# A hybrid decoder trunk: side tasks held back by VectorE's queue, and one small product in rounded form

## The chip, the cores and the metric

The kernel runs on one core of a Trainium2 chip. The metric is the device time of one execution in microseconds; the time given for a kernel is the median of several runs. A profiled execution, taken on the same core, gives the trace. Engines: TensorE (PE, with its weight loads PEld), VectorE (DVE), ScalarE (ACT), GpSimd (POOL) and SyncE (SP, which issues the DMAs).

## The reference

One layer over 256 tokens of 1024 channels. A normalised, conditioned `h` goes through one wide input projection; three mixers work on its parts (a matrix memory with a short convolution, a 31-tap convolution module, and a sparse attention), their outputs go through a projection each, are weighted by sigmoid gates and summed, and an output projection and a norm end it. The change touches the attention. Cut to that:

```python
def compress(t, j):                      # 15 blocks of 32 tokens, stride 16
    blk = ...                            # (15, G_C, 32 * 128), plus pe[j]
    return gelu(blk @ w1[j]) @ w2[j]
kc, vc = compress(k_cmp, 0), compress(v_cmp, 1)
# per block of queries, G_C = 2 groups of 4 heads:
s_c = einsum('bqgjd,bngd->bgjqn', qb, kc) * scale
p_c = masked_softmax(s_c, cmp_end <= t)
o_c = einsum('bgjqn,bngd->bqgjd', p_c, vc)      # the product that the change rewrites
... # o_s (selected blocks), o_w (window) likewise over 256 keys
return gb0 * o_c + gb1 * o_s + gb2 * o_w
```

## The kernel before

**Numbers.** The large products are done with float32 split in two rounded halves: `w_hi` is the weight cast to the rounded type `F32R` on ScalarE, `w_lo` the rest, subtracted on VectorE. A projection is three products, hi x hi, lo x hi and hi x lo. Smaller products, the attention's among them, run in plain float32.

**Order.** The kernel is written out once, in program order, by a planner (`Loom`, lines 74 to 250), which keeps for each engine the time until which it has given it work (`free`), with modelled costs. The main line issues TensorE's projections: `group_feat` (256 columns, output `ps_f`) and `tok` (512 columns, `ps_t`, two banks out of a ring of three). After every few matmuls it calls `weave` (line 206). That steps side tasks, which are Python generators: each runs to its next `yield`, which gives the planned time at which it may go on. Tasks have ranks: 0 for the weight splits, 1 for what the main line will want soon (the short convolutions, the heads of the matrix memory, the gates' sigmoids), and 2, the default of `spawn` (line 225), for the others: `u_gen`, the compression (`cmp_gen`), the small gates (`misc_gen`), the attention (`nsa_gen`, line 919), the tails of two branches (`branch_a`, line 1230, with `num` and `ga`; `branch_b`, line 1239, with `lsum`, `u` and `lsq`) and the output gate (`gate_gen`, line 712, with `a_raw`). The 31-tap convolution is the fill (line 212): it is stepped while VectorE's planned queue is under 600 ns beyond TensorE's position. `need` (line 232) forces a task to its end at once; the main line does so with the attention before the `cz` projections (line 1209), with each branch before its product (line 1287), and with the output gate before the last projection (line 1308).

**The weights' way.** Four raw buffers of 1 MB each are filled by DMA; side tasks that load (the compression and the output gate) take one of the four while they work.

**The attention's sum.** For each of 2 groups and 2 halves of the tokens, `nsa_gen` computes scores (`ps_s`), exponentials (`pm`), and scales them; `flips` (line 1002) then transposes the probabilities by blocks of 128 keys into a bank `pt` (`ps_p`), and copies it to `p_t`. For the 16 compressed keys it copies 16 rows to `ptc`, a tile whose other 112 rows were set to zero, and the product takes `vcmp[g]`, a tile filled in the same way by the compression (line 811), as its weights. All blocks are summed in one bank, `ps_o`, which is copied to `oc`.

**The branches' end.** After the `cz` projections the main line computes the gate of a branch (`mix_gate`, line 1258: `tok`, then VectorE adds a bias into `gs`), then the branch's product, in the order c, a, b.

Of the kernel before, what the change touches and what calls it, by code (L numbers as in the profile page):

```python
# [11 lines left out]
F32 = mybir.dt.float32  # L12
F32R = mybir.dt.float32r
AF = mybir.ActivationFunctionType
OP = mybir.AluOpType
# [52 lines left out]
RAWS, HIS, LOS = 4, 3, 3  # L68
GAP = 600.0
SLACK = 250.0  # L70
ROOM = dict(act=900.0, dve=900.0)


class Loom:
# [58 lines left out]
    def until(self, engine, *aps):  # L133
        return max(self.when(engine, a) for a in aps) + (SLACK if engine == "pe" else 0.0)

# [64 lines left out]
    def room(self, engine):  # L200
        return self.free[engine] - ROOM[engine]

# [2 lines left out]

    def weave(self):
        while True:
            task = next((t for t in self.tasks if t[0] <= self.now()), None)
            if task is None:
                break  # L210
            self.step(task)
        while self.fill and self.free["dve"] < self.now() + GAP:
            self.step(self.fill[0])
            if self.fill[0][2]:
                self.fill.pop(0)
# [49 lines left out]
def trunk(ctx: ExitStack, tc, xtok, crow, wada, wave0, wgrp, wmisc, w1, wbr, wout, par, vbias, out):  # L265
    nc = tc.nc
    const = ctx.enter_context(tc.tile_pool(name="const", bufs=1))
# [10 lines left out]
    act, dve, pe = [Line(loom, e, n) for e, n in ((nc.scalar, "act"), (nc.vector, "dve"), (nc.tensor, "pe"))]  # L278
    pool = nc.gpsimd
    until, weave, spawn, need, drop = loom.until, loom.weave, loom.spawn, loom.need, loom.drop  # L280
# [4 lines left out]
    def midt(name, shape):  # L285
        return mid.tile(shape, F32, name=name, tag="mid")
# [4 lines left out]
    def bank(name, kind="mm"):  # L291
        return loom.alloc(psum.tile([128, 512], F32, name=name, tag=kind, bufs=BANKS[kind]), kind, BANKS[kind])
# [10 lines left out]
    def flip(o, a):  # L303
        return pe.transpose(o, a, ident)
# [22 lines left out]
    def pc(name, i=0, n=1):  # L327
        return p_sb[:, PAR[name] + i:PAR[name] + i + n]
# [408 lines left out]
    ckv = ckb[:, 0].rearrange("p (a b c) -> p a b c", a=2, b=2)  # L737
    kk = [const.tile([128, 528], F32, name=f"kk{g}") for g in range(2)]
    vtok = midt("vtok", [128, 2, 2, 256])
    vcmp = [const.tile([128, 128], F32, name=f"vcmp{g}") for g in range(2)]  # L740
    for g in range(2):
        pool.memset(vcmp[g], 0.0)

    def cmp_gen(j):
        for g in range(2):
            c = ckv[:, j, g, :]
            src = bass.AP(tensor=c.tensor, offset=c.offset, ap=[list(c.ap[0]), [1, 32], [16, 15]])
            dve.tensor_tensor(blk[:, :, 16 * g:16 * g + 15], src,
                              pc("pe", 32 * j, 32)[:, :, None].broadcast_to([128, 32, 15]), op=OP.add)
        yield from loom.slot("sd")  # L750
        ps = bank("ps_c1", "sd")

        def load(c):
            w = rawt([128, 8, 256], "w1_raw")
            loom.load(nc.sync, w, w1[4 * j + c])
            return w

        yield from raw_slot()
        nxt = load(0)
        for c in range(4):  # L760
            if c < 3:
                yield from raw_slot()
            w, nxt = nxt, load(c + 1) if c < 3 else None
            yield until("pe", w, blk)
            for e in range(8):
                q = e % 4
                mm(ps[32 * q:32 * q + 32, 0:256], blk[:, 8 * c + e, :], w[:, e], c == 0 and e < 4,
                   c == 3 and e >= 4, tile_position=(0, 32 * q), skip_group_check=True)
            raw_free(w)
        part = ringt(work, [128, 256], "part", "mu", 1)  # L770
        yield until("act", ps)
        act.copy(part, ps[:, 0:256])
        drop(ps)
        yield until("pe", part)
        yield from loom.slot("sd")
        ps = bank("ps_c2", "sd")
        for f in range(2):
            mm(ps[:, 32 * f:32 * f + 32], part[:, 128 * f:128 * f + 128], gather4, True, True)
        hid = work.tile([128, 64], F32, name="hid", tag="hid")
        yield until("act", ps)  # L780
        act.copy(hid, ps[:, 0:64])
        drop(ps)
        yield until("dve", hid)
        t = work.tile([128, 64], F32, name="gt", tag="gt")
        dve.tensor_tensor(t, hid, hid, op=OP.mult)
        dve.tensor_tensor(t, t, hid, op=OP.mult)
        dve.scalar_tensor_tensor(t, t, 0.044715, hid, op0=OP.mult, op1=OP.add)
        yield until("act", t)
        act.activation(t, t, AF.Tanh, scale=0.7978845608028654)
        yield until("dve", t)  # L790
        dve.tensor_scalar(t, t, 0.5, 0.5, op0=OP.mult, op1=OP.add)
        dve.tensor_tensor(hid, hid, t, op=OP.mult)
        yield until("pe", hid)
        w2 = [pc("w2", (2 * j + f) * 128, 128) for f in range(2)]
        if j == 0:
            yield from loom.slot("sd")
            ps = bank("ps_kc", "sd")
            for f in range(2):
                mm(ps[:, 0:32], w2[f], hid[:, 32 * f:32 * f + 32], f == 0, f == 1)
            yield until("act", ps)  # L800
            for g in range(2):
                act.copy(kk[g][:, 384:400], ps[:, 16 * g:16 * g + 16])
            drop(ps)
        else:
            for g in range(2):
                yield from loom.slot("sd")
                ps = bank("ps_vc", "sd")
                for f in range(2):
                    mm(ps[0:16, 0:128], hid[:, 32 * f + 16 * g:32 * f + 16 * g + 16], w2[f], f == 0, f == 1)
                yield until("act", ps)  # L810
                act.copy(vcmp[g][0:16, :], ps[0:16, 0:128])
                drop(ps)

    blk = ckb[:, 1].rearrange("p (a b) -> p a b", a=32)
# [104 lines left out]
    def nsa_gen(qs, oc, ptc):  # L919
        for g in range(2):  # L920
            for t in range(2):
# [62 lines left out]
                if t == 0:  # L984
                    full = [pc_, pm[:, :, 0:128], pm[:, :, 128:256]]
                else:
# [3 lines left out]
                    full = [pc_, pm[:, :, 0:256], w]  # L990
# [11 lines left out]
                def flips(c, kind, kt):  # L1002
                    w = 16 if kind == 2 else 128
                    yield from loom.slot("sd")
                    pt = bank("ps_p", "sd")
                    for j in range(4):
                        flip(pt[0:w, 128 * j:128 * j + 128], pm[:, j, c:c + w])
                    yield until("act", pt)
                    if kind == 2:
                        act.copy(ptc[0:16, :], pt[0:16, :])  # L1010
                        drop(pt)
                        return vcmp[g], ptc
                    p_t = ringt(work, [128, 512], "p_t", "p_t", 2)
                    act.copy(p_t, pt)
                    drop(pt)
                    return vtok[:, kt, kind, 128 * g:128 * g + 128], p_t
# [107 lines left out]
    for n, ev in (("cks", evac_kk(True)), ("ckw", evac_kk(False))):  # L1124
        group_feat(n, 0, ev)
    group_tok("cv", 0, lambda t, ps: dve.tensor_tensor(vtok[:, t].rearrange("p a b -> p (a b)"), ps, vb_kv[:, 0:512],
                                                       op=OP.add))
# [1 line left out]
    for i in range(4):  # L1129
        group_feat("cq", i, evac_fn(lambda t: qs[:, t]))  # L1130
    oc = bigt("oc")
    ptc = const.tile([128, 512], F32, name="ptc")
    pool.memset(ptc, 0.0)

    def nsa_all():
        yield from loom.after(g_cmp, g_misc)
# [325 lines left out]
```

## Time and profile before

| | us |
|---|---|
| median of 3 runs | 511.48 (511.13 to 512.28) |
| profiled execution, its own time | 511.16 |
| its span | 509.4 |
| PE busy | 497.6 (98%) |
| PEld busy | 440.4 (86%) |
| DVE busy | 434.7 (85%) |
| ACT busy | 310.9 (61%) |

The span goes from the first instruction to the last; the time has a little more around it. Busy shares are averages over stages with different limits. Matmuls overlap in TensorE, so its busy time says less than the distance between the starts of neighbouring matmuls. A releaser, written `<-DVE gs`, is the engine and tile whose end let the instruction begin. Mean granted clock of TensorE over the span: 0.995 of its full speed.

### The profile page before, as it was taken

What the parts mean: (1) busy time and instruction counts of PE and PEld (TensorE: products, weight loads), DVE (VectorE), ACT (ScalarE), POOL (GpSimd) and SP (SyncE); (2) the same over time, 40 slices, a digit from 0 to 9 for tenths busy, and PEclk for the clock granted to TensorE, in tenths of its full rate; (3) what the DMA queues carried; (4) which work ended last, traced back from release to release, by engine and by line L of the source; (5) the groups of instructions that cost most, each with busy time, mean ns of one, the idle gap of its engine ahead of it and who ended that gap; (6) DMA issues with size and microseconds to landing.
All of it is one profiled execution on the core that took longest, in us unless ns stands there. A gap on an engine that the chain in (4) does not pass through costs nothing.

```text
span 509.4 us, 8567 instructions
## 1 busy us (share of the span) xinstructions
PE 497.6 (98%) x3258; PEld 440.4 (86%) x3258; DVE 434.7 (85%) x876; ACT 310.9 (61%) x524; POOL 7.3 (1%) x40
## 2 busy tenths in 40 slices
PE   8999999999999999999999999998999999999994
PEld 6999999799878989888898999996878888888883
DVE  4999799999999899899899987679998975756755
ACT  5656756335465858979497775666566844354442
POOL 4000000000000000000000000000000000000000
PEclk9999999999999999999999999998999999999999
DMA  7999954884774234404324247544657685455402
GB/s 262 382 406 356 406 223 156 330 323 167 279 300 167 95 154 160 170 8 167 134 109 167 84 144 271 206 166 165 224 182 297 247 314 215 174 196 215 169 0 82
DMA packets 18042, 105.32 MB, mean 207 GB/s; under 512 B 2129, under 2 KB 2257, under 8 KB 7890
## 3 DMA queue, kind: packets, MB, share of 16 engines
q1 hardware_dynamic: 18002, 104.79, 55.3%
q8 instruction: 25, 0.41, 0.3%
q14 instruction: 15, 0.12, 0.1%
HBM read 103.73 MB, written 1.05 MB: 206 GB/s over the span
## 4 chain that ended last, share of the span: by engine, by line
PE 91%; DVE 5%; DMA 1%; issue 1%; ACT 1%; DVEq 0%; SPq 0%; ACTq 0%
PE ps_f L165 35%; PE ps_t L165 29%; PE w L165 9%; PE ps_out L165 4%; PE ps_o L165 3%; PE ps_s L165 2%; PE ps_c L165 2%; DVE w_lo L165 1%; PE ps_p L165 1%; DMA x_sb<-in_xtok_dram 1%; PE ps_qk L165 1%; PE ps_n L165 1%; DVE u L165 1%; PE ps_heat L165 1%; DVE lsum L165 0%
## 5 line engine op out<-in xcount | busy, mean ns | idle before, releaser
L165 DVE TENSOR_TENSOR w_lo<-w_raw,w_hi 128x1024 fp32r<-128x1024 f32 x148 | 180.3, 1221 | 39.3 <-ACT w_hi L165 39.1
L165 ACT CAST w_hi<-w_raw 128x1024 fp32r<-128x1024 f32 x148 | 154.7, 1046 | 81.5 <-PE ps_t L165 55.0
L165 PE MATMUL ps_f<-h_hi,w_hi 128*128 128x256 f32 x512 | 131.0, 292 | 0.0
L165 PE MATMUL ps_f<-h_lo,w_hi 128*128 128x256 f32 x512 | 126.1, 283 | 0.0
L165 PEld LDWEIGHTS ps_f<-h_hi,w_hi 128*128 128x128 f32 x512 | 98.0, 191 | 2.9 <-issue 2.4
L165 PEld LDWEIGHTS ps_f<-h_lo,w_hi 128*128 128x128 f32 x512 | 98.1, 192 | 1.4 <-issue 1.0
L165 DVE SCALAR_TENSOR_TENSOR acc<-u,p_sb,acc 128x226 f32<-128x226 f32 (+28 forms) x232 | 93.1, 461 | 0.9 <-ACT acc L165 0.9
L165 PE MATMUL ps_f<-h_hi,w_lo 128*128 128x256 f32 x512 | 76.4, 288 | 0.0
L165 PEld LDWEIGHTS ps_f<-h_hi,w_lo 128*128 128x128 f32 x512 | 67.2, 191 | 2.0 <-issue 1.3
L165 PE MATMUL ps_t<-w_hi,h_hi 128*128 128x512 f32 x144 | 57.3, 398 | 2.0 <-DVE gs L165 2.0
L165 PE MATMUL ps_t<-w_hi,h_lo 128*128 128x512 f32 x144 | 56.6, 393 | 0.0
L165 PE MATMUL ps_t<-w_lo,h_hi 128*128 128x512 f32 x144 | 45.9, 400 | 0.0
L165 PEld LDWEIGHTS ps_t<-w_hi,h_hi 128*128 128x128 f32 x144 | 27.4, 190 | 8.3 <-DVE gs L165 2.5
L165 ACT ACT_TABLE_LOAD x25 | 32.1, 1283 | 1.2 <-PEq L1454 0.8
L165 PEld LDWEIGHTS ps_t<-w_lo,h_hi 128*128 128x128 f32 x144 | 26.9, 190 | 6.2 <-issue 0.8
L165 PEld LDWEIGHTS ps_t<-w_hi,h_lo 128*128 128x128 f32 x144 | 27.4, 190 | 5.4
L165 PE MATMUL w<-h_lo,w_hi 128*128 128x256 f32 x128 | 31.4, 283 | 0.0
L165 PE MATMUL w<-h_hi,w_lo 128*128 128x256 f32 x128 | 31.4, 283 | 0.0
L165 DVE SCALAR_TENSOR_TENSOR a_raw<-a_raw,cb 128x1024 f32<-128x1024 f32 x24 | 28.6, 1219 | 0.0
L165 PEld LDWEIGHTS w<-h_hi,w_lo 128*128 128x128 f32 x128 | 24.6, 192 | 0.0
L165 PEld LDWEIGHTS w<-h_lo,w_hi 128*128 128x128 f32 x128 | 24.6, 192 | 0.0
L165 ACT ACTIVATE pm<-pm,mx 128x16 f32<-128x16 f32 (+2 forms) x48 | 19.0, 401 | 0.3 <-DVE mx L165 0.3
(261 smaller groups left out, 707.8 us busy)
## 6 DMA issues: line engine op xcount, KB each, us to landing
w_raw<-in_wgrp_dram SPq DMA_DIRECT2D x50, 1024.0 KB, 4.8
w_raw<-in_wbr_dram SPq DMA_DIRECT2D x12, 1024.0 KB, 4.8
a_raw<-in_wada_dram SPq DMA_DIRECT2D x16, 512.0 KB, 6.8
w_raw<-in_wave_dram SPq DMA_DIRECT2D x16, 512.0 KB, 6.7
w_raw<-in_w_dram SPq DMA_DIRECT2D x8, 1024.0 KB, 4.8
a_raw<-in_wada_dram SPq DMA_DIRECT2D x4, 1024.0 KB, 4.8
w_raw<-in_wout_dram SPq DMA_DIRECT2D x4, 1024.0 KB, 4.8
vb_mg<-in_vbias_dram SPq DMA_DIRECT2D x3, 512.0 KB, 6.6
```

The source lines that it names most:

```text
L165: inst = self.pin(fn(*args, **kw))
```

## The change

First, `weave` no longer takes a task of rank 2 while the planner's VectorE is given work beyond 1500 ns after TensorE's position; tasks of rank 0 and 1, the fill and `need` are not affected. Second, the product of the compressed keys' probabilities with the compressed values is done with rounded operands, as one product. The rows of `vcmp` hold, at partitions 0, 32 and 64, the rounded values twice and their rest; those of `ptc` hold the rounded probabilities, their rest, and the rounded probabilities again. One product over all 128 partitions thus sums hi x hi, hi x lo and lo x hi. ScalarE writes the rounded copies (two instead of one), VectorE subtracts the rest out of the PSUM bank, and the task has a `yield` for VectorE in between.

```diff
+BACKLOG = 1500.0
@@ weave
-            task = next((t for t in self.tasks if t[0] <= self.now()), None)
+            full = self.free["dve"] > self.now() + BACKLOG
+            task = next((t for t in self.tasks if t[0] <= self.now() and not (full and t[3] == 2)), None)
@@
-    vcmp = [const.tile([128, 128], F32, name=f"vcmp{g}") for g in range(2)]
+    vcmp = [const.tile([128, 128], F32R, name=f"vcmp{g}") for g in range(2)]
     for g in range(2):
-        pool.memset(vcmp[g], 0.0)
+        pool.memset(vcmp[g].bitcast(F32), 0.0)
@@ cmp_gen
                 yield until("act", ps)
-                act.copy(vcmp[g][0:16, :], ps[0:16, 0:128])
+                for q in (0, 32):
+                    act.copy(vcmp[g][q:q + 16, :], ps[0:16, 0:128])
+                yield until("dve", vcmp[g])
+                dve.tensor_tensor(vcmp[g][64:80, :], ps[0:16, 0:128], vcmp[g][0:16, :], op=OP.subtract)
                 drop(ps)
@@ flips
                     if kind == 2:
-                        act.copy(ptc[0:16, :], pt[0:16, :])
+                        for q in (0, 64):
+                            act.copy(ptc[q:q + 16, :], pt[0:16, :])
+                        yield until("dve", ptc)
+                        dve.tensor_tensor(ptc[32:48, :], pt[0:16, :], ptc[0:16, :], op=OP.subtract)
                         drop(pt)
                         return vcmp[g], ptc
@@
-    ptc = const.tile([128, 512], F32, name="ptc")
-    pool.memset(ptc, 0.0)
+    ptc = const.tile([128, 512], F32R, name="ptc")
+    pool.memset(ptc.bitcast(F32), 0.0)
```

## Rows read from the trace of the kernel before

**Rows 1.** The page's busy time, share of the span and instructions of each engine.
```profile
PE 497.6 (98%) x3258; PEld 440.4 (86%) x3258; DVE 434.7 (85%) x876; ACT 310.9 (61%) x524; POOL 7.3 (1%) x40
```
**Rows 2.** Chain of waits, then TensorE in time: start us, us, what.
```profile
183.48 0.86 PE ps_o L165 x2
...
338.35 0.40 PE L165 MATMUL ps_t<-w_hi,h_hi 128*128 128x512 f32 x1
338.58 0.40 PE L165 MATMUL ps_t<-w_hi,h_lo 128*128 128x512 f32 x1
```
**Rows 3.** Who waited for whom: us in total, times, longest us.
```profile
PE ps_t L165 <- DVE gs L165: 2.0, 1, 2.0
...
PEld ps_o L165 <- ACT ptc L165: 0.2, 1, 0.2
```
**Rows 4.** Windows: length, busy of PE, PEld, DVE, ACT, POOL; clock, DMA share, GB/s.
```profile
351.70:353.75 2.05, 0.01 (x2) 0.00 (x1) 2.05 (x4) 0.66 (x2) 0.00 (x0) 1.00 0.35 68
353.75:357.27 3.52, 3.52 (x11) 2.85 (x11) 3.52 (x6) 2.70 (x4) 0.00 (x0) 0.52 0.62 258
...
357.27:379.20 21.93, 21.93 (x106) 18.22 (x105) 20.69 (x32) 13.93 (x18) 0.00 (x0) 1.00 0.60 216
...
388.00:454.00 66.00, 66.00 (x301) 54.93 (x300) 48.66 (x58) 36.92 (x46) 0.00 (x0) 1.00 0.61 231
```
**Rows 5.** Groups by form on ScalarE and VectorE: busy us, mean ns, idle before.
```profile
L165 ACT COPY ptc<-ps_p 16x512 f32<-16x512 f32 x4 | 2.3, 563 | 0.0
...
L165 ACT COPY vcmp<-ps_vc 16x128 f32<-16x128 f32 x2 | 0.5, 252 | 1.5 <-PE ps_vc L165 1.5
...
L165 DVE TENSOR_TENSOR cm<-cm 4x256 f32<-4x256 f32 x7 | 2.9, 413 | 0.2
...
L165 DVE TENSOR_TENSOR m_lo<-ps_mf,m_hi 128x512 fp32r<-128x512 f32 x4 | 2.7, 686 | 0.4 <-ACT m_hi L165 0.4
```
**Rows 6.** TensorE, then VectorE in time around the wait for `gs`.
```profile
348.83 0.39 PE L165 MATMUL ps_t<-w_hi,h_hi 128*128 128x512 f32 x1
...
351.10 0.61 PE L165 MATMUL ps_t<-w_lo,h_hi 128*128 128x512 f32 x2
...
348.36 1.22 DVE L165 TENSOR_TENSOR w_lo<-w_raw,w_hi 128x1024 fp32r<-128x1024 f32 x1
349.50 0.68 DVE L165 TENSOR_TENSOR ga<-ps_ht,ga 128x512 f32<-128x512 f32 x1
350.10 0.73 DVE L165 TENSOR_SCALAR num<-num,mv,hf__4126 128x256 f32<-128x256 f32 x2
350.75 1.21 DVE L165 TENSOR_TENSOR w_lo<-w_raw,w_hi 128x1024 fp32r<-128x1024 f32 x1
351.88 1.21 DVE L165 TENSOR_TENSOR u<-u,mu 128x1024 f32<-128x1024 f32 x1
353.02 1.27 DVE L165 TENSOR_TENSOR gs<-ps_t,vb_mg 128x512 f32<-128x512 f32 x2
```
**Rows 7.** Tile `ya_lo` (durations ns, first and last start us); the page's weight loads.
```profile
L165 PEld LDWEIGHTS ps_t<-w_hi,ya_lo x32: 187/188/192, 400.7 to 434.2; 128*128 128x128 f32 x32
...
L165 DVE TENSOR_TENSOR ya_lo<-ga,ya_hi x4: 684/686/687, 370.7 to 381.1; 128x512 fp32r<-128x512 f32 x4
...
w_raw<-in_wgrp_dram SPq DMA_DIRECT2D x50, 1024.0 KB, 4.8
```
**Rows 8.** VectorE's groups from 158 to 283; the attention's end and `cz`'s start in time.
```profile
L165 DVE SCALAR_TENSOR_TENSOR acc<-u,p_sb,acc 128x248 f32<-128x248 f32 (+28 forms) x102 | 40.8, 459 | 0.0
L165 DVE TENSOR_TENSOR w_lo<-w_raw,w_hi 128x1024 fp32r<-128x1024 f32 x30 | 36.5, 1217 | 1.0 <-ACT w_hi L165 1.0
...
267.19 2.35 DVE L165 TENSOR_TENSOR pm<-pm,sm 128x1024 f32<-128x1024 f32 x2
...
281.08 0.59 ACT L165 COPY oc<-ps_o 128x512 f32<-128x512 f32 x1
...
315.31 0.28 PE L165 MATMUL ps_f<-h_hi,w_hi 128*128 128x256 f32 x1
```

## Prediction

> **What bounds the kernel now.** I read the shares of busy time first, then who waited for whom on TensorE, then tables of short windows around each wait, and last the instructions in order of time there. TensorE (PE) is busy for 497.6 of 509.4 us [rows 1], VectorE (DVE) for 85%. A busy share alone could mislead, so look at the starts: two 512-column products of rounded (fp32r) operands start 0.23 us apart [rows 2], and the next ones follow without a gap. TensorE is therefore the bound nearly everywhere, and time is won in only two ways: by giving it less to do, or by closing a hole. After the start-up there is one hole worth the name: TensorE waited once for 2.0 us on VectorE's `gs` [rows 3]. In the window of that wait, 351.70 to 353.75, TensorE did 0.01 us of work while VectorE was busy without a break; in the 3.52 us behind it the granted clock was 0.52, the lower of the two levels (1.2 GHz), and it is 1.00 again from 357.27 on [rows 4]. The hole thus costs 2.05 us of standing still, and 3.52 x (1 - 0.52) = 1.69 us of slow work: 3.7 us.
>
> A rule of the Trainium skill speaks against this reading: "Perfetto Trace Analysis", Identifying the Most-Contended Engine, says that matmul busy time is no measure of TensorE's headroom, and that the busy share of weight loads should be taken beside the useful work. By that, 86% would leave 14% of the span as room, and a saving on one product could vanish in it. The starts 0.23 us apart, product after product, agree with the first reading and not with this one: an engine with room would leave gaps. By the one reading the sum is the one below, by the other it is rival B.
>
> **Part 2, the compressed keys' product with the values.** It runs four times (2 groups x 2 token halves). Each is a float32 product of 512 columns that appears as two records and takes 0.86 us on the chain of waits [rows 2]. After the change it is one rounded product of the same 512 columns over all 128 partitions (the unused ones hold zeros, as before); 512 columns of that kind take 0.23 us. Saved: 4 x (0.86 - 0.23) = 2.5 us of TensorE. As nothing but TensorE's own work ends these stretches, I count all of it. Bounds: 0 if the place is filled by a new wait, 2.5 if not; I take 2.5.
>
> Added on ScalarE (ACT): a second copy of 16x512, four times at 0.56 us, and a second of 16x128, twice at 0.25 us: 2.7 us [rows 5]. Added on VectorE: four subtractions 16x512 out of PSUM into a rounded tile. The trace has none with 16 partitions; the nearest is `m_lo`, the same operands on 128 partitions, 0.69 us. Few partitions don't make it much cheaper: 4x256 still takes 0.41 us, over half of that for half the columns. So 4 x 0.69 and two of 128 columns at 0.4 or less: 3.5 us; bounds 1.6 us (the 4x256 price four times, nothing for the small ones) and 3.6 us. What hides both: ScalarE is busy 61% of the span, and on VectorE the work displaces convolution steps, a fill that runs only when nothing else is queued. If that cover were gone, the 3.5 us would stand in front of splits, as a further 3.5 us of holes at most. New wait: the product waits for VectorE's subtraction rather than ScalarE's copy. Behind it on TensorE stand the projections `ps_f`; a misjudged VectorE would hold them, perhaps 0.5 us each time, 0 to 2 us for four. I take 0, since the planner places a TensorE instruction 250 ns after the operand is due, and the product waited for ScalarE's `ptc` only 0.2 us in all four rounds [rows 3]. The two memsets change only the type under which they are written; no DMA is added or moved.
>
> **Part 1, the gate on low-rank tasks.** Before, any side task whose due time has come is stepped at each pause of the matmuls. Now one of rank 2 (the default: the compression, the small gates, the attention, the two branch tails, the output gate) isn't stepped while the planner has over 1.5 us of VectorE work queued beyond TensorE's position. Ranks 0 (weight splits) and 1, the fill, and everything forced by `need` go on. Look at the hole. The first bank of the gate product was complete when the last six matmuls began at 348.83; TensorE needs that bank back after those of 351.10, about 351.7. The evacuation `gs` reads as many columns as `m_lo` (0.69 us), so it should start by 351.0; it starts at 353.02 [rows 6]. In front of it, behind the split already running, VectorE does `ga` (0.60, by the distance of the starts), `num` (0.65), a split `w_lo` (1.13), and `u` minus the mean (1.14). Three of the four are rank 2, of the branch tails: 2.39 us. VectorE's backlog then is 353.02 - 348.83 = 4.2 us, far above 1.5, so these are what the gate holds. Without the three, `gs` starts at 350.6, is done at 351.3, and the hole is gone, with the clock's drop: 3.7 us gained. If only the last is held, it starts at 351.9 and the hole is 0.9 us. But the gate lets a step through at any backlog below 1.5, and one step can bring 1.1 us more (as `u` does), and a split 1.14 on top. So the queue met by `gs` lies between 1.5 and 3.8 us; it may reach 2.2 (351.0 - 348.83) without harm. The ends are 0 and 3.7 us gained; below nothing, the same hole might come twice, 3.7 us lost. I take 3.3: the hole shrinks to where TensorE shows no drop, with 0.4 us left over.
>
> What is late next: the held work moves into 357 to 379, where VectorE is 94% busy (20.69 of 21.93), so the gate will stay near its threshold there, and then past 388, where it has 66 - 48.7 = 17 us of room [rows 4]. Branch a's last `ya_lo` starts at 381.1, and its product's weight loads begin at 400.7 [rows 7]: 19 us to give away for some 5 us of held work. The output gate's task holds one of four raw buffers while it waits, which leaves three for the weights; a load of 1 MB lands in 4.8 us [rows 7] and feeds 24 products, 24 x 0.23 = 5.5 us.
>
> **Sum.** Against the profiled execution: 511.16 - 2.5 - 3.3 = 505.4 us. The median of the three runs is 0.3 above that execution, so 505.7.
>
> **Rivals.**
> A, the hole stays or moves. For it: 94% busy VectorE right behind, and steps that pass at 1.4 us; against it: 2.4 us of the 4.2 in front of `gs` is of the gated kind. Time 511.5 - 2.5 = 509.0, down to 507 with half a hole. The gate doing nothing, because the planner never sees its backlog, gives the same 509.0.
> B, TensorE has hidden room and the rounded product saves nothing; the hole still goes: 511.5 - 3.3 = 508.2.
> C, slower: the attention comes late. It is rank 2, and from 158 to 283 VectorE is full: 30 splits take 36.5 us and 102 convolution steps 40.8 us [rows 8]. The fill stops near 0.6 us (its own bound) plus a pair of steps at 0.46 us, so at 1.5, just at the threshold; each split laid on it can close the gate for its own length: at most 36.5 us in all. To that comes the longer chain of part 2, 4 x (0.56 + 0.69 + about 1 us of queue) = 9 us. The last copy into `oc` starts at 281.08, and the attention is forced to its end where the `cz` projections begin, at 315.31: 33.6 us to spare. I expect a third of the bound, 12 + 9 = 21 us, so it holds. Past 34 us of delay, the last round's chain (from its last scaling at 267.2 to 281.7, 14 us, of which TensorE itself needs some 6 for five products at 0.86 and its transposes) runs with nothing beside it: 8 us of hole, with 1.7 us at the lower clock behind it as above. Time 509.0 + 9 or 10 = 518.5, or 515 if the first hole goes all the same.
> D, no change: smaller new holes (the product's wait, buffers held longer by paused tasks) eat the gain: 511.5.
>
> **Chances.** The forecast 0.52, its own range 503.6 to 507; A 0.22; B 0.05; C 0.13; D 0.08. What can be told from no change here is 0.2%, 1.0 us. Faster: 0.52 + 0.22 + 0.05 = 0.79; same: 0.08; slower: 0.13. The range begins at 503.6 (both terms whole, 511.5 - 2.5 - 3.7 = 505.3, less the 1.0 us by which a measurement may be off and some shorter waits) and goes to 511.5, which takes in A, B and half of D.
>
> **What would show it.** Right: four single records of `ps_o<-ptc,vcmp` of about 0.4 us with 0.23 us to the next start; no TensorE wait on `gs` above 0.5 us and a granted clock of 1.00 near 350; `lsum`, `num`, `u` later than before, `gs` within 2 us of its bank. Wrong: a wait on `gs` or `merged` of 1 us or more anywhere from 335 to 400 (A); a TensorE span that shrinks by less than the records saved (B); a hole at the start of `cz`, with `oc` or `pm` as its releaser (C); TensorE waiting on `ptc`, or weight loads waiting on a DMA (D).

## The result: slower by 0.6%

The changed kernel takes 515.0 us (514.7 to 515.5) against 511.7 us of the kernel before, run beside it: a ratio of 1.0064, 95% interval 1.0048 to 1.0081. The prediction had 505.7 and a range to 511.5, so it was wrong in sign. The profiled execution took 514.95 us, its span is 513.2.

The page's busy line of the changed kernel stands almost as in [rows 1]: TensorE works as long as before, in a longer span.

```profile
PE 497.1 (97%) x3254; PEld 441.0 (86%) x3254; DVE 438.3 (85%) x882; ACT 309.3 (60%) x526; POOL 7.3 (1%) x40
```

Who waited for whom on TensorE (us in total, times, longest) shows a changed picture. The hole at `gs` of [rows 3] is gone as forecast. In its place stand two waits for a weight split `w_lo`, which the kernel before did not have, and two for `ptc`.

```profile
PE ps_f L166 <- DVE w_lo L166: 5.4, 2, 4.0
PE ps_o L166 <- DVE ptc L166: 1.3, 2, 0.9
...
PE ps_t L166 <- DVE gs L166: 0.2, 1, 0.2
```

The steps of the small product: ScalarE's casts, VectorE's subtraction, the product (durations in ns, least, median, most, then first and last start).

```profile
L166 ACT CAST ptc<-ps_p x8: 559/574/577, 186.9 to 316.9; 16x512 fp32r<-16x512 f32 x8
L166 DVE TENSOR_TENSOR ptc<-ps_p,ptc x4: 680/680/680, 188.9 to 318.3; 16x512 fp32r<-16x512 f32 x4
...
L166 PE MATMUL ps_o<-ptc,vcmp x4: 391/498/499, 189.7 to 319.0; 128*128 128x512 f32 x4
```

The product has four records of 0.39 to 0.50 us, where [rows 2] had two records and 0.86 us for each. The subtraction takes 0.680 us on 16 partitions, nearly the 0.686 of 128 in [rows 5]. So the price of each step by itself was near.

To see where the time went, cut the execution at two marks: the first and the last start of the projections `ps_f`, and the last start of the output product `ps_out`. They stand in the tiles' first and last starts; the last copy into `oc` is the end of the attention.

```profile
L166 PE MATMUL ps_f<-h_hi,w_hi x512: 278/283/682, 62.4 to 345.0; 128*128 128x256 f32 x171
...
L166 PE MATMUL ps_f<-h_hi,w_lo x512: 277/283/582, 64.3 to 346.1; 128*128 128x256 f32 x171
```

```profile
L166 PE MATMUL ps_out<-w_hi,m_lo x32: 388/389/397, 483.8 to 505.9; 128*128 128x512 f32 x32
```

The same in the kernel before:

```profile
L165 PE MATMUL ps_f<-h_hi,w_hi x512: 278/283/682, 61.6 to 337.2; 128*128 128x256 f32 x171
...
L165 PE MATMUL ps_f<-h_hi,w_lo x512: 274/283/682, 63.5 to 338.2; 128*128 128x256 f32 x171
...
L165 PE MATMUL ps_out<-w_hi,m_lo x32: 388/389/397, 480.0 to 502.1; 128*128 128x512 f32 x32
```

And the copies into `oc` in the changed kernel:

```profile
L166 ACT COPY oc<-ps_o x4: 562/577/588, 192.4 to 319.5; 128x512 f32<-128x512 f32 x4
```

The first stretch, 62.4 to 346.1, is 283.7 us; before it was 276.6 (61.6 to 338.2). The last, to 505.9, is 159.8 us; before it was 163.9. So the change lost 7.1 us in the first and won 4.1 us in the last; 0.8 us more passed before the first stretch began, in these two executions. The attention ends at 319.5; before it ended at 281.1 [rows 8].

The loss in the first stretch lies around the two waits for `w_lo` (windows: length, busy time of PE, PEld, DVE, ACT, POOL; granted clock, DMA share, GB/s).

```profile
293.85:295.26 1.41, 0.00 (x0) 0.00 (x0) 1.41 (x3) 1.40 (x3) 0.00 (x0) 1.00 0.00 0
298.40:302.36 3.96, 0.00 (x0) 0.00 (x1) 3.73 (x9) 1.09 (x2) 0.00 (x0) 0.75 0.00 0
302.36:307.20 4.84, 4.84 (x22) 4.84 (x23) 4.84 (x7) 1.72 (x3) 0.00 (x0) 0.50 0.79 247
307.20:340.00 32.80, 32.78 (x254) 30.21 (x253) 26.91 (x48) 18.88 (x28) 0.00 (x0) 1.00 0.48 173
```

In 1.41 and 3.96 us TensorE did nothing, and in the 4.84 us behind the second its clock was 0.50, the lower level (1.2 GHz), as behind the old hole in [rows 4]. What VectorE and ScalarE did there, in order of time (start, us, what; in brackets the idle time ahead of it and what ended it):

```profile
287.34 1.04 ACT L166 CAST w_hi<-w_raw 128x1024 fp32r<-128x1024 f32 x1
288.39 1.28 ACT L166 ACT_TABLE_LOAD   x1
289.69 0.63 ACT L166 ACTIVATE ga<-ga 128x512 f32<-128x512 f32 x1
...
290.80 0.36 ACT L166 COPY num<-ps_n 128x256 f32<-128x256 f32 x1
291.18 1.28 ACT L166 ACT_TABLE_LOAD   x1
292.47 0.51 ACT L166 ACTIVATE pm<-pm,mx 128x256 f32<-128x256 f32 x1
...
293.09 1.28 ACT L166 ACT_TABLE_LOAD   x1
```

```profile
291.19 0.43 DVE L166 BATCH_NORM_STATS2 st<-ps_n 128x6 f32<-128x256 f32 x1 [4.32 <-ACT num L166]
...
291.76 2.31 DVE L166 SCALAR_TENSOR_TENSOR acc<-u,p_sb,acc 128x236 f32<-128x236 f32 x6
293.99 1.22 DVE L166 TENSOR_TENSOR w_lo<-w_raw,w_hi 128x1024 fp32r<-128x1024 f32 x1
295.13 3.12 DVE L166 SCALAR_TENSOR_TENSOR acc<-u,p_sb,acc 128x239 f32<-128x239 f32 x8
298.16 0.22 DVE L166 TENSOR_TENSOR pm<-pm,keep 128x64 f32<-128x64 f32 x1
...
301.09 1.22 DVE L166 TENSOR_TENSOR w_lo<-w_raw,w_hi 128x1024 fp32r<-128x1024 f32 x1
```

On ScalarE the last exponentials of the late attention (`pm`) alternate with the heads' activations (`ga`, `zb`, `sz`), and each change of function brings a table load of 1.28 us: three from 288.39 to 294.37. The copy `num` of the matrix memory stands in that queue until 290.80. VectorE's next instruction in its queue, the statistics `st`, needs `num`: VectorE stands for 4.32 us. What is queued behind it comes late: six convolution steps, a split (first hole), eight steps and the attention's scaling (`pm`, `sm`), and only at 301.09 the split that ends the second hole. The table loads themselves are not more than before: four start between 280 and 325 us in either kernel (21 in the whole span, 25 before). New are the exponentials: four of them stand on ScalarE between this copy of `num` and the one ahead of it (284.95), none between the same two copies before. There VectorE waited 1.7 us for `num`.

### The profile page after: what moved, and what is told of

The parts are those of the page before. It is cut to its first block, busy times and chain, and to the rows that moved or that the text cites. A ratio compares the mean times of both kernels' runs of the same rounds, so it can differ in the third digit from the quotient of the medians.

```text
span 513.2 us, 8574 instructions
## 1 busy us (share of the span) xinstructions
PE 497.1 (97%) x3254; PEld 441.0 (86%) x3254; DVE 438.3 (85%) x882; ACT 309.3 (60%) x526; POOL 7.3 (1%) x40
## 4 chain that ended last, share of the span: by engine, by line
PE 81%; DVE 9%; DMA 5%; ACT 3%; issue 2%; SPq 0%; DVEq 0%; ACTq 0%
PE ps_f L166 32%; PE ps_t L166 30%; PE w L166 5%; PE ps_out L166 4%; DMA w_raw<-in_wave_dram 4%; DVE w_lo L166 3%; PE ps_s L166 2%; DVE acc L166 2%; PE ps_c L166 2%; PE ps_o L166 2%; DMA x_sb<-in_xtok_dram 1%; PE ps_p L166 1%; PE ps_qk L166 1%; ACT w_hi L166 1%; PE ps_n L166 1%
## 5 line engine op out<-in xcount | busy, mean ns | idle before, releaser
L166 ACT ACT_TABLE_LOAD x21 | 26.9, 1283 | 1.1 <-PEq L1462 0.8
```

Of the source, the lines that this page charges most:

```text
L166: inst = self.pin(fn(*args, **kw))
```

## The experiments

All times are medians; each ratio is to the kernel before, run beside it. First stretch, last stretch and the start of the last `oc` copy are read in each trace as above.

| run | us | ratio to before (95%) | first | last | `oc` |
|---|---|---|---|---|---|
| before | 510.8 to 511.7 | | 276.6 | 163.9 | 281.1 |
| changed | 515.0 | 1.0064 (1.0048-1.0081) | 283.7 | 159.8 | 319.5 |
| e1 product only | 519.2 | 1.0152 (1.0133-1.0171) | 284.0 | 164.3 | 306.3 |
| e2 gate only | 509.1 | 0.9952 (0.9938-0.9966) | 278.5 | 159.8 | 305.8 |
| e3 attention free | 513.6 | 1.0048 (1.0032-1.0064) | 282.5 | 159.9 | 304.3 |
| e4 attention held | 520.3 | 1.0176 (1.0158-1.0194) | 284.9 | 165.7 | 320.0 |
| e5 product placed later | 515.8 | 1.0088 (1.0073-1.0103) | 280.2 | 164.4 | 308.0 |
| e6 no rest | 511.6 | 1.0012 (1.0003-1.0022) | 276.9 | 164.3 | 296.3 |
| e7 tails held | 507.2 | 0.9925 (0.9912-0.9937) | 276.7 | 159.8 | 280.7 |
| e8 statistics later | 513.6 | 1.0054 (1.0039-1.0069) | 283.2 | 159.8 | 317.3 |
| e9 work only | 518.2 | 1.0142 (1.0125-1.0160) | 279.8 | 166.6 | 299.7 |
| e10 first term only | 511.6 | 1.0007 (0.9999-1.0016) | 274.7 | 166.3 | 292.6 |
| e11 same, old order | 510.8 | 0.9992 (0.9980-1.0004) | 276.3 | 163.9 | 281.2 |
| e12 tails held, flips early | 513.4 | 1.0045 (1.0030-1.0060) | 283.8 | 159.8 | 313.9 |
| e13 tails held, work only | 511.5 | 1.0023 (1.0002-1.0044) | 279.7 | 159.8 | 300.5 |
| e14 tails held, first term | 505.6 | 0.9895 (0.9882-0.9908) | 274.7 | 159.8 | 293.5 |
| e15 tails held, product | 515.0 | 1.0071 (1.0059-1.0083) | 283.8 | 159.8 | 305.6 |
| e16 tails held, subtractions | 509.1 | 0.9960 (0.9948-0.9972) | 278.6 | 159.8 | 299.3 |
| e17 tails held, attention late | 507.4 | 0.9929 (0.9917-0.9942) | 276.7 | 159.8 | 294.7 |
| e18 tails held, later still | 514.4 | 1.0067 (1.0055-1.0078) | 283.8 | 159.8 | 324.1 |

### Which part, and which held task (e1 to e4)

The parts alone, and the gate on some tasks (a flag `held` in `spawn`, asked in `weave`).

```diff
e1  -BACKLOG = 1500.0   +BACKLOG = 1e9
e2  (the old product, with the gate)
e3  + and not (full and t[3] == 2 and t[4])       # t[4]: held, by default True
    -g_nsa = spawn(nsa_all())   +g_nsa = spawn(nsa_all(), held=False)
e4  -def spawn(self, gen, rank=2):   +def spawn(self, gen, rank=2, held=False):
    -g_nsa = spawn(nsa_all())   +g_nsa = spawn(nsa_all(), held=True)
```

Expected of e1:

> The changed kernel with the gate taken out (its bound set out of reach), the rounded product kept. Theory 1 (the gate makes the attention late: held, its last exponentials fall among the SiLU and sigmoid work that ScalarE does for the ao projections, VectorE's head statistics wait behind them, and TensorE waits 5.4 us for w_lo): the attention is on time again, its last copy into oc starts below 292 us; TensorE loses nothing on w_lo; the wait on gs of about 2 us is back; time 511.7 - 2.5 + about 1 for waits on ptc = 510 (509 to 511). Theory 2 (the longer chain of the product makes it late, the gate is innocent): last oc copy beyond 305, holes on w_lo, time 513 or more.

Expected of e2:

> The kernel before with the gate of 1500 ns, the product in float32 as before. Theory 1: the attention ends some 30 us later than before, with a hole on w_lo of several us between 290 and 310 and the tail shorter by 4 us; time 511.7 - 4.1 + 8 = 515.5 (513 to 518). Theory 2: no hole there, the tail's gain alone: 507.6.

Expected of e3:

> The changed kernel, but the attention is not held by the gate (all other rank 2 tasks are). Theory 1: last oc copy below 292 us, no wait on w_lo, no wait on gs above 0.5 us; time 515.0 - 5.4 - 2.4 (clock behind the hole) = 507, or 506 if waits on ptc go too (505 to 508). Theory 2: 515, as the changed kernel.

Expected of e4:

> The changed kernel, but only the attention is held; the compression, the small gates, the branch tails and the output gate are free. Theory 1: the holes on w_lo between 290 and 310 stay and the wait on gs of 2 us is back: 515.0 + 3.7 = 518.5 (516 to 521). Theory 3 (the delay comes from holding the compression and the small gates, before the attention starts): the attention is on time, 510.

My first theory, that the gate on the attention made all of the loss, fell: the product alone costs 8.0 us, and the gate alone gains 2.1. In e1 TensorE waits for VectorE's `ptc` 5.7 us in three waits, and for `gs` as before. Holding the attention decides which loss comes: e4, with the attention alone held, has the changed kernel's two waits for `w_lo` (5.4 us), and e3, with it alone free, has none of them but 5.6 us of waits for `ptc`. The column of the last stretch is the clean part: 159.8 or 159.9 wherever the branches' tails are held, 163.9 or more where they are not.

### The gate where it pays (e7)

```diff
-    g_a, g_b, g_gate = spawn(branch_a()), spawn(branch_b()), spawn(gate_gen())
+    g_a, g_b, g_gate = [spawn(x, held=True) for x in (branch_a(), branch_b(), gate_gen())]
```
(with `held=False` for all others, and the old product)

> The gate on the small gates' and the two branches' tails alone (branch_a, branch_b, gate_gen), with the old product. The stretch from the last final-stage group's start to the end was 163.9 us before and 159.8 to 159.9 in the three kernels with these tails held. Theory A: the gate's worth lies in that stretch alone, and the middle is as before: 511.1 - 4.1 = 507.0 (506.3 to 508); the gate on everything measured 509.1, since it also delayed the middle by 1.9 us. Rival: the tails' gain is only given with the attention or the compression held as well, and this is within 0.3 of the kernel before or of 509.1.

It came out at 507.2, all of the gain in the last stretch (163.9 to 159.8), none lost in the first. This version beats both kernels, the one before by 0.75%. Against e2 it also shows what holding the attention and the other tasks costs: 278.5 - 276.7 = 1.8 us.

### The wait on the subtraction (e5, e6, e12)

```diff
e5  -yield until("pe", p_t)
    +yield until("pe", p_t) + (3000.0 if b == len(blocks) - 1 else 0.0)
e6  -yield until("dve", ptc)
    -dve.tensor_tensor(ptc[32:48, :], pt[0:16, :], ptc[0:16, :], op=OP.subtract)
e12 +last = yield from flips(*blocks[-1])      # the compressed block's, ahead of the others
     ... its product stays the last; tails held as in e7
```
(e5 and e6 without the gate)

Expected of e5:

> The new product without the gate (as in the product alone, 519.2), but the compressed block's product is placed 3000 ns later in TensorE's order: the wait of TensorE on VectorE's subtraction into ptc was 2.29, 2.94 and 0.45 us there, so with 3 us more the subtraction should have been done. Theory A (the product waits in TensorE's in-order queue for a VectorE step that the planner believes done): the waits on ptc go from 5.7 us to below 0.5, and the time to the kernel before less the saving on TensorE, 511.1 - 4 x (0.86 - 0.23) = 508.6; between 507.5 and 510.5. Theory B (the added copies and subtractions themselves cost, since ScalarE or VectorE is the bound there, whoever waits): they are all still there, so 515 or more.

Expected of e6:

> The new product without the gate, and without the four subtractions that write the probabilities' rest into ptc (this leaves out the third term of the product, and the output misses it); the casts on ScalarE and the rounded matmul stay. Theory A: with no VectorE step between the probabilities and the product, there is no wait on ptc that ends on VectorE, and the time is 508.6 (507.5 to 510.5), as with the later placing. Theory B, ScalarE's part (the second casts, 4 x 0.57 us, cost): the time stays at 513 or more, with the waits on ScalarE. VectorE's own time of the subtractions (4 x 0.68 us) goes too, so a time below 507.5 would say that VectorE is the bound in that stretch.

Expected of e12:

> Gate on the branches' tails and the small gates alone (507.2 with the old product), the new product, and the compressed block's probabilities turned, cast and subtracted ahead of the other blocks, while its matmul stays the last: two to four blocks (1.2 us of TensorE each and what lies between) pass before TensorE needs ptc. Theory A: no wait on ptc of over 0.3 us, time 507.2 - 2.5 = 504.7 (503.5 to 506.5). Theory B (the work): 507.2 + 3 = 510 or more though the wait is gone. Theory D (a plan made anew opens other holes): 507 to 511 with the holes at other tiles.

Each time the wait on `ptc` shrank or went (5.7 to 2.1 us in e5; none on VectorE in e6 and none at all in e12), and each time more was left over than the wait's theory allowed: 515.8, 511.6 and 513.4 for 508.6, 508.6 and 504.7. In e12 the task stops for the subtraction ahead of all blocks, the attention ends at 313.9, and the waits come at `w_lo` (2.7 us, as in the changed kernel), `w_hi` (1.3) and `mx` (1.3). So taking the wait away did not give the time back. By the first stretch e6 is the nearest to it (276.9, where e1 has 284.0), but it leaves out the wait and the four subtractions together.

### The work and the saving by themselves (e9, e10, e11)

```diff
e9  (old product)  act.copy(ptc[0:16, :], pt[0:16, :])
    +act.copy(idle[64:80, :], pt[0:16, :])
    +yield until("dve", idle)
    +dve.tensor_tensor(idle[32:48, :], pt[0:16, :], ptc[0:16, :], op=OP.subtract)   # vcmp alike
e10 (rounded product)  -for q in (0, 64): ...  -dve.tensor_tensor(ptc[32:48, :], ...)
    +act.copy(ptc[0:16, :], pt[0:16, :])                                            # vcmp alike
    (e10 and e11 without the gate)
e11 e10, and in the planner's costs: F32R and not args[2].tensor.name.startswith("ptc")
```

Expected of e9:

> The kernel before with the old product, to which the added work of the new one is joined without any use of it: the second casts on ScalarE (4 x 0.57 and 2 x 0.26 us) and the subtractions on VectorE (4 x 0.68, 2 x 0.28 us) go to a tile that nothing reads. TensorE's product is as dear as before and waits for no VectorE step. Theory A (what costs is TensorE's wait for the subtraction): 511.2, within 1 us. Theory B (what costs is the work itself: VectorE is busy 37.3 to 38.2 of each 40 us between 160 and 280 us, so 3.3 us more of it there push all that TensorE waits for): 511.2 + 3 or more, 514 to 517, with new waits of TensorE on VectorE in the middle. The product alone cost 8.0, and 5.5 of it was not the wait's length of 5.7 less 2.5 saved, so a result between would share the loss.

Expected of e10:

> The rounded product with its first term alone: one cast of the probabilities and one of the values, as in the kernel before, no second casts and no subtractions (this leaves out the two rest terms). TensorE saves 4 x 0.63 us = 2.5 us and nothing is added anywhere. The planner knows the cheaper matmul and places what follows anew. Theory A and B alike: 511.2 - 2.5 = 508.7. Theory D (TensorE's saving is not the kernel's: VectorE and ScalarE are next, and a plan made anew opens holes elsewhere): 510.5 to 513, with holes at other tiles.

Expected of e11:

> As the one with the first term alone, but the planner is told the old cost for this product, so that every engine has its instructions in exactly the order of the kernel before; only the four matmuls are cheaper. Theory A and B: 508.7, and the stretch from the first to the last final-stage group 276.6 - 2.5 = 274.1. Theory D splits here: if VectorE is the next bound, 510.5 or more again; if it is only the plan made anew that costs, 508.7 here and more in the kernel with the plan made anew.

Work that nobody uses costs 7.0 us, and the cheaper product alone gains nothing to be measured. But the stretches say more than the totals: the work lengthens the first by 3.2 us and the cheaper product shortens it by 1.9, while the last stretch, in which neither is done, grew by 2.7 and 2.4 us because the tails, held by nothing, fell differently. e11 keeps every instruction in the old order; there the saving in the first stretch is 0.3 us instead of 1.9, and TensorE has new waits in that stretch, on VectorE and ScalarE:

```profile
PE ps_s L166 <- DVE mx L166: 0.7, 2, 0.5
PE ps_qk L166 <- ACT qk L166: 0.6, 1, 0.6
```

They come 3 to 4 us behind three of the four products: at `mx` near 187 and 223 us, at `qk` near 283. TensorE gets there earlier by what it saved, and waits.

### The same on a base that stands still (e13 to e16)

With the tails held the last stretch is 159.8 us in all, so the parts can be read from the first.

```diff
e13 e9 on the base of e7
e14 e10 on the base of e7
e15 the whole product on the base of e7
e16 e13 without the second casts:  -act.copy(idle[64:80, :], pt[0:16, :])
```

Expected of e13:

> The branches' tails and small gates held, the old product, and the added work (second casts and subtractions) to a tile that nothing reads. Theory B (VectorE is full between 160 and 300 us, so its work there costs its length): 507.2 + 3.2, the growth of the first stretch that the same work gave without the gate (276.6 to 279.8), = 510.4 (509.5 to 511.5); the 2.7 us more of the last stretch then belonged to the tails that nothing held. Theory A (only the wait costs): 507.2. If the whole 7.0 us was the work's: 514.

Expected of e14:

> Tails held, the rounded product with its first term alone (the two rest terms are left out), the planner knowing the cheaper matmul. If TensorE's saving is the kernel's: 507.2 - 1.9 (the first stretch went from 276.6 to 274.7 without the gate) = 505.3, or with the whole 2.5 us 504.7. If VectorE takes over what TensorE saves: 507 or more.

Expected of e15:

> Tails held and the whole new product, the attention not held. If the parts add up (work +3.2, saving -1.9, waits on ptc +6.1, these from the first stretch of 284.0 with the product alone against 279.8 with the work alone): 507.2 + 7.4 = 514.6 (513.5 to 516), with waits on ptc of 4 to 6 us. If the gate on the tails takes VectorE's backlog away in the middle too, so that ptc is on time: 508 to 509.

Expected of e16:

> As the one with the work alone, but without the second casts: only the subtractions on VectorE (4 x 0.68, 2 x 0.28 us = 3.3 us) to a tile that nothing reads. VectorE as the bound: as dear as with the casts, 510.4 (within 0.7). ScalarE as the bound (its casts, 2.8 us): 507.2 to 508.

Read from e7's first stretch of 276.7: the subtractions cost 1.9 us (e16, 278.6; their own length is 4 x 0.68 + 2 x 0.28 = 3.3), the second casts 1.1 more (e13, 279.7), the cheaper product gains 2.0 (e14, 274.7), and the whole costs 7.1 (e15, 283.8). (e14 is the lowest of all, but without the rest terms it is no candidate.) So neither engine alone is the bound: the steps on VectorE cost over half their length, those on ScalarE (2.8 us) over a third. In e13 TensorE's waits account for 2.0 of the 3.0 us: these two (in e7 `pm` alone, 0.3 us), and 0.4 us each for VectorE's `mx` and ScalarE's `qk`.

```profile
PE ps_p L166 <- DVE pm L166: 0.8, 2, 0.5
PE ps_o L166 <- ACT ptc L166: 0.7, 1, 0.7
```

In e16 the trace names only 0.2 us more of waits than in e7, so where its 1.9 us went is not shown. Nor do the runs part the work from what comes with it: each added step is a stop of the attention's task, the plan is made anew, and the last copy into `oc` moves from 280.7 to 299.3 and 300.5. The medians agree with the stretches within 0.7 us but for e13, 4.3 us above e7, whose twelve runs spread from 509.9 to 515.6; why that kernel alone is so unsteady is left open.

What the whole has beyond work and saving is the wait. In e15, TensorE's waits:

```profile
PE ps_o L166 <- DVE ptc L166: 5.7, 3, 2.9
```

The longest of the three, in order of time on TensorE, ScalarE and VectorE:

```profile
230.75 1.02 PE L166 MATMUL ps_o<-p_t,vtok 128*128 128x512 f32 x2
234.71 0.79 PE L166 MATMUL ps_o<-ptc,vcmp 128*128 128x512 f32 x1 [2.94 <-DVE ptc L166]
```

```profile
230.02 1.16 ACT L166 CAST ptc<-ps_p 16x512 fp32r<-16x512 f32 x2 [0.22 <-PE ps_p L166]
```

```profile
227.68 2.76 DVE L166 SCALAR_TENSOR_TENSOR acc<-u,p_sb,acc 128x241 f32<-128x241 f32 x7
230.36 1.65 DVE L166 SCALAR_TENSOR_TENSOR acc<-pre,p_sb,acc 128x253 f32<-128x253 f32 x4
231.94 1.21 DVE L166 TENSOR_TENSOR w_lo<-w_raw,w_hi 128x1024 fp32r<-128x1024 f32 x1
...
233.97 0.68 DVE L166 TENSOR_TENSOR ptc<-ps_p,ptc 16x512 fp32r<-16x512 f32 x1
```

The second cast ends at 231.2. VectorE is then in its convolution and `qk` steps (eleven `acc` since 227.68); the subtraction, next in line but for a split and two `qk` steps, starts at 233.97. TensorE has finished what stood ahead of the product at 231.77 and waits 2.94 us. The planner places the product 250 ns after VectorE's planned end; by the wait, VectorE was some 3 us behind the plan. The windows of the two longer holes and what follows each:

```profile
183.95:186.23 2.28, 0.00 (x1) 0.00 (x1) 2.22 (x5) 1.86 (x4) 0.00 (x0) 1.00 0.44 183
186.23:190.00 3.77, 3.77 (x14) 3.34 (x15) 2.83 (x9) 2.00 (x3) 0.00 (x0) 0.55 0.00 0
...
231.77:234.71 2.94, 0.00 (x2) 0.00 (x1) 2.85 (x5) 0.00 (x0) 0.10 (x1) 0.90 0.38 45
234.71:237.00 2.29, 2.29 (x5) 1.81 (x6) 0.00 (x0) 1.46 (x3) 0.00 (x0) 0.50 0.81 340
237.00:241.00 4.00, 4.00 (x20) 3.45 (x19) 1.48 (x11) 2.06 (x4) 0.00 (x0) 0.93 0.10 39
```

Holes of 2.28 and 2.94 us and a third of 0.44 are 5.7 us of standing still; the lower clock behind them costs 3.77 x 0.45 + 2.29 x 0.50 + 4 x 0.07 = 3.1 us. Together 8.8, less the saving of 2.0, is 6.8 of the 7.1 us. The sum has no room for the work's own 3.0 us besides; I take it that VectorE catches up while TensorE stands, which no run shows.

### The late attention by itself (e8, e17, e18)

e15 and the changed kernel take the same time, though in the second the waits on `ptc` are 1.3 us and those on `w_lo` 5.4. The difference is the gate on the attention. e8 takes one link out of the chain seen above; e17 and e18 delay the attention's last round, with the old product and the tails held.

```diff
e8        act.copy(num[:, 2 * h + t], pn[:, 0:256])
         +yield until("dve", num[:, 2 * h + t])
          dve.bn_stats(st[:, h, t], pn[:, 0:256])
e17, e18  for t in range(2):
         +    if g == 1 and t == 1:
         +        yield loom.now() + 6000.0       # e18: 18000.0
```

Expected of e8:

> The changed kernel, but the statistics on num in the final heads are placed as a step of their own once ScalarE's copy of num is due, so that VectorE's queue is not blocked behind a late ScalarE (4.32 us at 287 to 291 in the changed kernel, just before the two holes on w_lo of 1.41 and 3.97 us). Theory C (in the changed kernel the loss is that chain: late attention, its exponentials on ScalarE, VectorE blocked by the statistics, TensorE without w_lo): the w_lo waits go from 5.4 us to below 1.5, the clock after them stays up, and the time is 508 to 510. Rival (VectorE is behind by work, not by that one wait): the w_lo waits stay above 3 us and the time above 513.

Expected of e17:

> Tails held, the old product, and the attention's last round put off by 6 us of the planner's clock, which sets its last product where the kernel with the whole new product has it (some 230 matmul rows before the end of the groups, the end of the attention near 305 us instead of 281). If lateness up to there is harmless (in the gate alone the attention ended at 305.8 and TensorE waited 0.7 us on w_lo): 507.2, within 1. If lateness is what the product costs: 512 to 515.

Expected of e18:

> The same with 18 us, which sets the last product where the changed kernel has it (the end of the attention near 320 us). Theory C (its exponentials then fall among the heads' silu and the table loads on ScalarE, and TensorE waits for w_lo or w_hi): waits of 4 us or more at 285 to 305, a low clock behind them, 511 to 515. Rival (the holes need the product's work too): 507 to 509.

In e8 TensorE's wait on `w_lo` fell to 0.4 us, but a wait on ScalarE's cast took its place, and at most 1.4 us were won (0.5 in the first stretch):

```profile
PE ps_f L166 <- ACT w_hi L166: 4.0, 1, 4.0
```

So VectorE standing behind `num` was a link, not the cause; ScalarE itself was late. e17 and e18 test the lateness alone. With the last copy at 294.7 the time is that of e7, to 0.1 us. (I had aimed at 305. Whether 305 is harmless too is not shown: e2, with 305.8, waits 0.7 us on `w_lo`, and its first stretch is 1.8 us longer, but other tasks are held there as well.) At 324.1 it is 7 us slower, with no work added at all. TensorE waits once:

```profile
PE ps_f L166 <- DVE w_lo L166: 4.0, 1, 4.0
```

ScalarE in that stretch:

```profile
290.26 1.28 ACT L166 ACT_TABLE_LOAD   x1
291.56 0.51 ACT L166 ACTIVATE pm<-pm,mx 128x256 f32<-128x256 f32 x1
...
292.18 1.28 ACT L166 ACT_TABLE_LOAD   x1
293.47 0.47 ACT L166 ACTIVATE sz<-ps_f,p_sb 128x256 f32<-128x256 f32 x1
293.85 1.04 ACT L166 CAST w_hi<-w_raw 128x1024 fp32r<-128x1024 f32 x1
```

```profile
280.00:295.00 15.00, 15.00 (x116) 14.52 (x115) 11.28 (x29) 14.90 (x32) 0.00 (x0) 1.00 0.40 141
```

From 280 to 295 ScalarE is busy 14.90 of 15 us. Exponentials of 0.51 us stand between activations of other functions, with a table load on either side: two, 2.6 us, for one exponential here, and eleven loads from 287.8 to 315.8. The cast `w_hi` at 293.85 stands behind them, and so does the copy `num` at 294.84. VectorE then shows the changed kernel's chain again: it stands for `num`, does eight convolution steps, and the split that ends TensorE's wait comes at 300.64.

```profile
295.25 0.43 DVE L166 BATCH_NORM_STATS2 st<-ps_n 128x6 f32<-128x256 f32 x1 [3.94 <-ACT num L166]
...
296.36 3.18 DVE L166 SCALAR_TENSOR_TENSOR acc<-u,p_sb,acc 128x249 f32<-128x249 f32 x8
...
300.64 1.22 DVE L166 TENSOR_TENSOR w_lo<-w_raw,w_hi 128x1024 fp32r<-128x1024 f32 x1
```

One thing differs: e18 has twelve table loads between 280 and 325 us, the changed kernel only four. So e18 shows that lateness alone can cost 7 us, by the same chain; it does not show that table loads make the loss in the changed kernel.

The Trainium skill, "ScalarE: Activation LUTs", What ACT_TABLE_LOAD costs, gives such a switch 1283 ns and a drain of some 1380 ns more, 2.66 us together. The load's 1.28 us agrees. The drain is not to be seen here: in the changed kernel the cast before a load ends at 288.38, the load begins at 288.39 and ends at 289.67, and the next activation begins at 289.69.

## Why the prediction was wrong, step by step

**Part 1, the gate: right, and near in size.** I took 3.3 us from the hole at `gs`, with 3.7 as the upper end; the last stretch became 4.1 us shorter, `gs` waits 0.2 us, and the granted clock from 340 to 400 is 1.00. e7 shows the same gain with only the tails held. The rival that the hole stays fell.

**Part 2, the saving: right in kind, 2.0 us for 2.5.** e14 shows it in the first stretch. Rival B, room hidden in TensorE, fell: with the planner told of the cheaper product and the tails held, 2.0 us of it show in the stretch and 1.6 in the medians (507.2 to 505.6). e11 adds a condition that I had not seen: in the old order TensorE ran into the other queues and kept 0.3 us.

The rule that I weighed there, of the Trainium skill's "Perfetto Trace Analysis", Identifying the Most-Contended Engine, would have left 14% of the span as room by the weight loads. e14 speaks against it for this kernel: a saving of 2.5 us on matmuls won 2.0 in its stretch; and what e11 lost of it went into waits for other engines.

**Part 2, the cover and the wait put at nothing: the first step that failed.** I wrote "What hides both: ScalarE is busy 61% of the span, and on VectorE the work displaces convolution steps", and for the new wait "I take 0, since the planner places a TensorE instruction 250 ns after the operand is due". Both zeros were wrong. The first read a stretch by the average of the span: from 160 to 280 VectorE is nearly full, which I used myself for rival C and forgot here, and ScalarE, 61% of the span, is 92% busy in a third of it (kernel before; windows as above):

```profile
200.00:240.00 40.00, 40.00 (x247) 34.52 (x246) 37.75 (x101) 36.61 (x82) 0.20 (x2) 1.00 0.37 132
```

The added work, with a product that does not read it, costs 3.0 us (e13), more than the saving and within the "3.5 us of holes at most" that I had named for the case without cover. The second trusted the planner's clock for an engine that is late against it; the product's wait for ScalarE, 0.2 us in [rows 3], told nothing of a wait for VectorE's queue. The waits and the clock behind them measured 8.8 us (e15), where I had priced "0 to 2 us for four"; in the changed kernel itself, where the attention is held, the waits were 1.3 us. By these numbers the product could not pay in this plan: its work alone eats the saving.

**The delay of the attention put at nothing: the step that failed in the changed kernel itself.** For rival C I wrote "I expect a third of the bound, 12 + 9 = 21 us, so it holds": any delay below 33.6 us was to cost nothing, and the forecast has no term for it. The delay was 38.4 us. Nor does the bound hold: in e12 the attention is 32.8 us late (313.9 for 281.1), and TensorE already waits 2.7 us for `w_lo` and 1.3 for `w_hi`. In the changed kernel the holes came not at `cz` but from 293 to 302, where the exponentials met the heads' activations on ScalarE, an engine that the rival did not name. The price there: holes of 1.41 and 3.97 us, 1.3 us at `ptc` and 4.84 x 0.50 = 2.4 us of clock make 9.1, less 2.0 saved, 7.1, the whole growth of the first stretch. (The sum has nothing for the added work, nor for the other tasks held, so that it comes out to a tenth says little.) e18 shows the same 7.1 without the product. The figure of 515 that I gave for C "if the first hole goes all the same" is what was measured, but by luck: C priced one hole of 8 us at `cz` and 1.7 us of clock, and what came were two holes and a wait elsewhere. The delay I had set by a third of a bound, with nothing to measure it.

**The two losses replace each other.** Where the attention is not held (e15), the product meets VectorE's backlog and waits 5.7 us for `ptc`; where it is held (changed), it waits 1.3 us, but the attention comes so late that it meets the heads on ScalarE. Both ways cost 7.1 us in the first stretch. Their being equal to a tenth is not explained by any run; I take it for chance.

**What stays open.** Why e12, whose product waits for nothing, has its attention at 313.9 and not at 305 was not separated from its early flips. From what delay on lateness costs time, between 294.7 (e17) and 313.9 (e12), was not measured. How much of the cost in e13 and e16 is the work and how much the new order was not separated either. Why e13 is so unsteady is not known. And a form of the product that spares the casts or the subtraction was not tried.

## What to carry to other kernels

Price added work on a second engine by that engine's load in the very stretch, not by its share of the span: where VectorE was 93 to 95% busy, 3.3 us of added steps there cost 1.9, the new order included (e16). An operand that moves from one engine to another changes whose queue the product waits in; look at how late that queue runs against the plan, not at the wait for the old one. And hold back only those tasks whose delay is free: holding the tails gained 4.1 us, holding the attention as well put its exponentials among the heads' activations on ScalarE, and VectorE and then TensorE waited behind them.

## What the runs showed of the hardware that I had not expected

- A subtraction of 512 columns out of PSUM takes 0.680 us on 16 partitions and 0.686 on 128; on ScalarE a cast of 16 x 512 takes 0.574. I had expected few partitions to cost about the same; that the two are so close is new.
- Behind an idle stretch of 1.41 us the granted clock stayed at 1.00 (295.26 to 298.40), while those of 2.28, 2.94 and 3.96 us were followed by 0.55, 0.50 and 0.50, and that of 2.05 us in [rows 4] by 0.52. It was 1.00 again from 190.00 and 307.20 on, 3.8 and 4.8 us behind the end of the hole.
- The table load at 288.39 in the changed kernel takes 1.28 us, and the next activation follows at once, with 0.02 us between.
